# First norm's shift and scale: both vectors through TensorE, in four lots of features

## The chip, the cores and the metric

The kernel runs on one core of one Trainium2 chip. The metric is the device time of one execution in microseconds; of several runs the median is quoted. The engines are TensorE (PE, its weight loads PEld), VectorE (DVE), ScalarE (ACT), GpSimd (POOL) and SyncE (SP), which issues the transfers.

## The reference, cut to what matters

Two layers of a diffusion backbone, on 512 latent tokens `x` and 256 context tokens `ctx` of 1024 features. Each layer is an FFN, a mixer and a second FFN, each between two norms. In front of each of them stands a norm with a shift and a scale, which are vectors made from a conditioning vector (one for latent tokens, one for context):

```python
s_lat, s_ctx = silu(c), silu(c_ctx)[None]
m_l = (s_lat @ w_ada[l] + b_ada[l]).reshape(B, 9, D)   # D = 1024
m_c = (s_ctx @ w_ada[l] + b_ada[l]).reshape(1, 9, D)

def pre_mod(x, g, m, slot):       # slot 0: m[:, 1] is the scale, m[:, 0] the shift
    return rmsnorm(x, g) * (1 + m[:, None, 3 * slot + 1]) + m[:, None, 3 * slot]

def ffn_sublayer(x, m, slot, g_pre, g_post, wg, wu, wd):
    h = pre_mod(x, g_pre, m, slot)
    y = (silu(h @ wg) * (h @ wu)) @ wd
    return post_residual(x, y, g_post, m, slot, 0.5)
```

Shift and scale of layer 0, slot 0 are the first two of the 9 x 1024 columns of `w_ada[0]`. They are needed before the first FFN can start, and the change is about them alone.

## The kernel before, in words

Features lie on the partitions: `X[k]`, k = 0 to 7, holds 128 features of all 768 tokens. Tokens go in three groups: context `G_C` (256), and the latent halves `G_A` and `G_B` (256 each). Every large product is done in three matmuls of rounded numbers: weights and activations are split into a high part and a low part (`whi`/`wlo`, `zh`/`zl`), and `mm3` (lines 515 to 522) adds high x high, high x low and low x high.

The opening is `begin` (line 245), a generator that `ffn` (line 524) advances step by step between its own statements. It loads `G_A`, then lot 0 of the weights, `G_B`, lot 1. A lot `q` is 256 of the 1024 features, that is the two k tiles 2q and 2q+1. For each lot it makes shift and scale, and then the normed tiles `z` of those two k for `G_A` and `G_B` (`z_tile`, line 465: VectorE scales, ScalarE adds the shift and writes `zh` and a full copy into `y`, VectorE or GpSimd subtracts to get `zl`).

- The scale goes through TensorE (line 311): 8 matmuls in f32 with the two silu columns as the stationary operand and 256 weight columns moving, into one bank of 2 x 256. ScalarE copies the row (line 327), two transposes turn it into columns (line 330), VectorE adds the bias and folds in the norm's gain (lines 332, 333).
- The shift goes through VectorE: `ada_dot` (line 243) multiplies transposed weights `wat` (features on the partitions) with `srow`, the silu vectors spread over all partitions, and sums along the row. A lot has two k, two conditioning vectors, and two pieces of each row, so eight dots, each followed by the read of the accumulator; 32 dots in all.

`srow` is made in `consts` (lines 208 to 214) by 16 matmuls of broadcast silu columns with the identity, and four copies. The background vectors of later norms (`ada_bg`, line 353; `pump`) use it too, with the same `ada_dot` on 1024 columns.

The weights of the shift land in `y[0]` to `y[4]` and in the buffers that later hold `gh` and `gl`; those of the scale land in the `raw` ring (four buffers, shared with the FFN's weight tiles) for lots 0 and 3, and in buffers of later z tiles for lots 1 and 2. The transfers are written in pieces: 16 for the shift (rows of 1 to 3 KB) and 10 for the scale (rows of 1 KB).

`ffn` then loads the gate and up tiles of the first two of its 22 feature tiles (`loads(0)`, `loads(1)`, one after lot 0's step, one after lot 1's) and does their products for the latent tokens by k as the z tiles come (`part`, line 676), k 0 to 3, 4 and 5, 6 and 7, then evacuates. After that the context is loaded, normed, and its products done (line 715). `combine` (line 550) forms sums and differences of the normed tokens on VectorE, with which most of the other feature tiles are multiplied (`fast`, line 588).

The order of instructions in each engine's queue is not the order of the text: `TileContext(nc, schedule_with_timeline_sim=True)` has a planner choose it from the dependences, the free buffers, and its own estimate of each instruction's time; the order in the text is the priority. On the chip each engine then takes its queue in order.

Of the kernel before, what the change touches and what calls it, by code (L numbers as in the profile page):

```python
# [5 lines left out]
F32 = mybir.dt.float32  # L6
# [8 lines left out]
P = 128  # L15
# [19 lines left out]
class K:  # L35
# [136 lines left out]
    def consts(self):  # L172
        nc, d = self.nc, self.d
        cp = self.cp = self.pool("const")
        self.sm = self.pool("small")
        cm = cp.tile([P, CM_COLS], F32, name="cm")
        nc.sync.dma_start(cm, d["cm"])
        o = CM_OFF
        self.ident = cm[:, o["ident"] : o["ident"] + P]
        self.LE = cm[:, o["le"] : o["le"] + P]  # L180
        self.GE = cm[:, o["ge"] : o["ge"] + P]
        self.LT = cm[:, o["lt"] : o["lt"] + P]
        self.GT = cm[:, o["gt"] : o["gt"] + P]
        self.C1 = cm[:, o["c1"] : o["c1"] + P]
        self.C2 = cm[:, o["c2"] : o["c2"] + P]
        self.M1 = cm[:, o["m1"] : o["m1"] + 32]
        self.M2 = cm[:, o["m2"] : o["m2"] + 32]
        cols = cp.tile([P, COLS], F32, name="cols")
        nc.sync.dma_start(cols, d["cols"])
        c = lambda n, w, l=0: cols[:, CO[n] + l * w : CO[n] + (l + 1) * w]  # L190
        self.c = c
        self.tab = cp.tile([P, NL], F32, name="tab")
        nc.sync.dma_start(self.tab, d["tab"])
        self.I32 = cp.tile([P, 32], F32, name="i32")
        nc.vector.reduce_sum(self.I32, self.ident.rearrange("p (b c) -> p c b", b=4), axis=AX)
        self.ones = cp.tile([P, P], F32, name="ones")
        nc.vector.memset(self.ones, 1.0)
        self.mhalf = cp.tile([P, 24], F32, name="mhalf")
        nc.vector.memset(self.mhalf, -0.5)
        self.phalf = cp.tile([P, 24], F32, name="phalf")  # L200
        nc.vector.memset(self.phalf, 0.5)
        cs = cp.tile([P, KT, 2], F32, name="cs")
        nc.sync.dma_start(cs, d["cs"])
        self.s = cp.tile([P, KT, 2], F32, name="s")
        nc.scalar.activation(self.s, cs, AF.Silu)
        self.M, self.scol, self.pg = {}, {}, {}

        self.srow = cp.tile([P, 2, 1024], F32, name="srow")
        for v in range(2):
            for h in range(2):  # L210
                ps = self.bank("srow")
                for j in range(4):
                    self.nc.tensor.matmul(ps[:, j * P : (j + 1) * P], self.s[:, 4 * h + j, v : v + 1].to_broadcast([P, P]), self.ident, start=True, stop=True)
                nc.scalar.copy(self.srow[:, v, h * 512 : (h + 1) * 512], ps)


# [20 lines left out]
        self.nc.sync.dma_start(raw, self.d["wat"][l, part, k])  # L237
        return raw

    def ada_dot(self, out, w, v, a, b, start=0.0, keep=False):  # L240

        dst = self.fp.tile([P, 1024], BF16, tag="adot", name="adot", bufs=1)[:, : b - a] if keep else w
        self.nc.vector.tensor_tensor_reduce(out=dst, in0=w, in1=self.srow[:, v, a:b], scale=1.0, scalar=start, op0=ALU.mult, op1=ALU.add, accum_out=out)  # L243

    def begin(self):

# [20 lines left out]
            return r  # L267

        m = {part: self.cp.tile([P, KT, 2], F32, name=f"m0_0_{part}") for part in range(2)}
        sh = self.cp.tile([P, KT, 2], F32, name="sh0")  # L270

        room = list(self.y[:5])
        for j in range(4):
            room += [self.fp.tile([P, NT], F32, tag=f"g{x}{j}", name="land") for x in "hl"]
        KS = [(0, 3), (3, 6), (6, 8)]

        PIECES = [[(0, 0, 768)], [(0, 768, 1024), (1, 0, 512)], [(1, 512, 1024)]]
        w0, w1 = {}, {}

        def load_q(q):  # L280
            cs = lambda part: slice(part * 1024 + q * 256, part * 1024 + (q + 1) * 256)
            for piece in PIECES:
                t, o = room.pop(0), 0
                for j, a, b in piece:
                    w = t[:, o : o + b - a]
                    nc.sync.dma_start(w, self.d["wat"][0, 0, 2 * q + j][:, a:b])
                    w0.setdefault(2 * q + j, []).append((w, a, b))
                    o += b - a
            if q in (1, 2):
                z = 2 * q + 2  # L290
                land = [(a, b, self.zps[q % 2].tile([P, NT], F32, tag=t, name="zland", bufs=1)) for (a, b), t in zip(KS, (f"zh{z}", f"zl{z}", f"zh{z + 1}"))]
            else:
                land = [(a, a + 4, self.wp.tile([P, 1024], F32, tag="raw", name="abraw", bufs=4)) for a in (0, 4)]
            for a, b, t in land:
                w = t[:, : (b - a) * 256].rearrange("p (k c) -> p k c", c=256)
                nc.sync.dma_start(w, self.d["w_ada"][a * P : b * P, cs(0)].rearrange("(k p) c -> p k c", p=P))
                for k in range(a, b):
                    w1[q, k] = w[:, k - a]

        load_x(G_A)  # L300
        load_q(0)
# [2 lines left out]
        yield  # L304
        for q in range(4):
            d = slice(2 * q, 2 * q + 2)
            ps = self.bank("adaps")
            if 0 < q < 3:
                load_q(q + 1)
            for k in range(KT):  # L310
                nc.tensor.matmul(ps[0:2, 0:256], self.s[:, k], w1[q, k], start=k == 0, stop=k == KT - 1)
            for k in (2 * q, 2 * q + 1):
                for v in range(2):
                    start = 0.0
                    for w, a, b in w0[k]:
                        self.ada_dot(sh[:, k, v : v + 1], w, v, a, b, start, keep=v == 0)
                        start = sh[:, k, v : v + 1]
            if q == 0:
                squares(G_A)
                squares(G_B)  # L320
            if q in (1, 2):
                z = 2 * q + 2
                self.zh[z] = self.zps[q % 2].tile([P, NT], F32R, tag=f"zh{z}", name=f"zh{z}", bufs=1)
                self.zl[z] = self.zps[q % 2].tile([P, NT], F32R, tag=f"zl{z}", name=f"zl{z}", bufs=1)
                self.zh[z + 1] = self.zps[q % 2].tile([P, NT], F32R, tag=f"zh{z + 1}", name=f"zh{z + 1}", bufs=1)
            row = self.sg("row")[0:2, 0:256]
            nc.scalar.copy(row, ps[0:2, 0:256])
            pt = self.aux("adapt")
            for j in range(2):
                nc.tensor.transpose(pt[:, 2 * j : 2 * j + 2], row[:, j * P : (j + 1) * P], self.ident[0:2, 0:2])  # L330
            b = lambda part: self.c("b_ada", KT, part)[:, d].unsqueeze(2).to_broadcast([P, 2, 2])
            nc.vector.tensor_tensor(out=m[1][:, d], in0=pt[:, 0:4].rearrange("p (d v) -> p d v", v=2), in1=b(1), op=ALU.add)
            nc.vector.scalar_tensor_tensor(out=m[1][:, d], in0=m[1][:, d], scalar=1.0, in1=self.c("norm_pre", KT, 0)[:, d].unsqueeze(2).to_broadcast([P, 2, 2]), op0=ALU.add, op1=ALU.mult)
            nc.vector.tensor_tensor(out=m[0][:, d], in0=sh[:, d], in1=b(0), op=ALU.add)
            if q == 0:
                self.M[0, 0, 0], self.M[0, 0, 1] = m[0], m[1]
                self.scol[0, 0] = m[1]
                R = {g: factor(g) for g in (G_A, G_B)}
            for g in (G_A, G_B):
                for k in (2 * q, 2 * q + 1):  # L340
                    self.z_tile(0, 0, g, R[g], k)
            yield
        load_x(G_C)

        def rest():
            squares(G_C)
# [6 lines left out]
    def ada_bg(self, l, slot, parts, vecs):  # L353


        raw = self.cp.tile([P, 3, KT, 2], F32, name=f"raw{l}_{slot}_{parts[0]}")

        def col(pi, k, w):
            for v in vecs:
                self.ada_dot(raw[:, pi, k, v : v + 1], w, v, 0, 1024, keep=v != vecs[-1])  # L360

        def fin():
            if len(vecs) == 1:
                self.nc.vector.tensor_copy(raw[:, : len(parts), :, 1], raw[:, : len(parts), :, 0])
            self.ada_cols(l, slot, raw, parts)

        for pi, part in enumerate(parts):
            for k in range(KT):
                dma = lambda a=(l, 3 * slot + part, k): self.ada_dma(*a)
                self.bg.append((dma, lambda w, a=(pi, k): col(*a, w)))  # L370
        self.bg.append((None, fin))
# [1486 lines left out]
def pack(i):  # L1858
# [4 lines left out]
    o["x"] = A(np.stack([xt[:, :, g[0] : g[0] + g[1]].transpose(1, 0, 2) for g in GROUPS]))  # L1863
    o["cs"] = A(np.stack([i["c"][0], i["c_ctx"]], -1).reshape(KT, P, 2).transpose(1, 0, 2))

    o["w_ada"] = A(i["w_ada"][0, :, 1024:2048])
    o["wat"] = A(i["w_ada"].transpose(0, 2, 1).reshape(2, 9, KT, P, 1024))
    T = lambda a, w: a.reshape(-1, w, P).transpose(2, 0, 1).reshape(P, -1)
    cols = dict(
# [146 lines left out]
```

## Time and profile before

| | us |
|---|---|
| median of 3 runs | 3329.84 |
| lowest, highest | 3324.64, 3330.06 |
| the profiled execution | 3321.82 |
| its span, first to last instruction | 3320.0 |

TensorE is busy 3058.4 us of the span, VectorE 2562.9, ScalarE 1377.4 and GpSimd 1345.7. All times in the rows below count from the start of the span. In rows of a timeline the first two numbers are the start and the duration, x8 is a run of eight merged instructions, and in brackets stands the idle time of the engine before it with what ended it. In windows the numbers of each engine are its busy time, then come the granted clock of TensorE as a share of 2.4 GHz (0.50 is 1.2 GHz), the busy share of the transfer engines and what they moved. In rows of groups a bar separates shape and count from the busy time, the mean of one in ns, and the idle time before.

### The profile page before, as it was taken

The page shows a single profiled execution, that of the slowest core. Times are in us where ns is not written, and L with a number is a line of the kernel's source. Part 1 is how long each engine was busy: PE and PEld are TensorE (multiplying, and loading weights), DVE is VectorE, ACT ScalarE, POOL GpSimd, SP SyncE. Part 2 cuts the span into 40 slices and gives each one's busy share as a digit, 9 for nine tenths or more (in the row PEclk, how much of TensorE's full clock was granted, in tenths as well). Part 3 has the DMA queues.
Part 4 walks back from the last instruction along what each step waited for, and adds up shares of the span by engine and source line. Part 5 has one row for each costly group of instructions (what it writes and reads, how often), then busy time and mean ns, then how long its engine had stood idle before and what let it go on. Part 6 is the DMA issues. An engine that isn't in the chain of part 4 may idle for free. (4 is left out here: it accounts for less than half of the span.)

```text
span 3320.0 us, 53695 instructions
## 1 busy us (share of the span) xinstructions
PE 3058.4 (92%) x20836; PEld 2785.7 (84%) x20836; DVE 2562.9 (77%) x4337; ACT 1377.4 (41%) x2600; POOL 1345.7 (41%) x1060
## 2 busy tenths in 40 slices
PE   7899999889889998999998899999989788989998
PEld 4799989878787798999998798999877676788998
DVE  7888887777778959677777977777677879776777
ACT  4333223544445644322234432223454346544343
POOL 5322122544655765222215511221544546753233
PEclk8999999889999899999999999999989899989999
DMA  6233333222310122323324233332322310224233
GB/s 221 101 122 122 107 127 117 94 73 54 97 64 10 51 86 81 108 91 107 101 73 158 82 109 114 121 127 89 104 98 64 88 46 17 91 90 134 96 106 98
DMA packets 149816, 318.68 MB, mean 96 GB/s; under 512 B 38185, under 2 KB 79529, under 8 KB 149561
## 3 DMA queue, kind: packets, MB, share of 16 engines
q1 hardware_dynamic: 149560, 315.25, 28.9%
q8 instruction: 163, 2.67, 0.3%
q14 instruction: 93, 0.75, 0.1%
HBM read 285.17 MB, written 30.03 MB: 95 GB/s over the span
## 5 line engine op out<-in xcount | busy, mean ns | idle before, releaser
L94 POOL TENSOR_TENSOR wlo<-wraw,whi 128x1024 fp32r<-128x1024 f32 (+1 forms) x228 | 580.3, 2554 | 1357.5 <-ACT whi L93 1304.9
L93 ACT CAST whi<-wraw 128x1024 fp32r<-128x1024 f32 (+2 forms) x482 | 469.5, 978 | 692.0 <-PE ps L776 338.5
L519 PE MATMUL ps<-zh,whi 128*128 128x256 f32 (+1 forms) x1208 | 389.5, 331 | 25.2 <-DVE sg L547 13.3
L608 PE MATMUL ps<-zh,whi 128*128 128x384 f32 (+1 forms) x1216 | 392.2, 323 | 8.0 <-DVE sg L547 4.5
L609 PE MATMUL ps<-zl,whi 128*128 128x384 f32 (+1 forms) x1216 | 392.1, 322 | 2.5 <-DVE zl L586 2.5
L610 PE MATMUL ps<-zh,wlo 128*128 128x384 f32 (+1 forms) x1216 | 390.8, 322 | 0.0
L520 PE MATMUL ps<-zl,whi 128*128 128x256 f32 (+1 forms) x1208 | 382.9, 327 | 5.0 <-DVE zl L477 5.0
L775 PE MATMUL ps<-gh,whi 128*128 128x512 f32 (+1 forms) x1008 | 349.5, 354 | 21.3 <-ACT gh L618 18.9
L776 PE MATMUL ps<-gl,whi 128*128 128x512 f32 (+1 forms) x1008 | 338.3, 352 | 17.3 <-DVE gl L619 17.3
L522 PE MATMUL ps<-zh,wlo 128*128 128x256 f32 (+1 forms) x1208 | 351.1, 324 | 0.0
L94 DVE TENSOR_TENSOR wlo<-wraw,whi 128x1024 fp32r<-128x1024 f32 (+1 forms) x254 | 298.1, 1175 | 31.3 <-ACT whi L93 29.9
L778 PE MATMUL ps<-gh,wlo 128*128 128x512 f32 (+1 forms) x1008 | 293.3, 348 | 0.0
L519 PEld LDWEIGHTS ps<-zh,whi 128*128 128x128 f32 x1208 | 236.8, 199 | 56.8 <-DVE sg L547 14.0
L520 PEld LDWEIGHTS ps<-zl,whi 128*128 128x128 f32 x1208 | 238.3, 198 | 24.5 <-DVE zl L477 6.1
L775 PEld LDWEIGHTS ps<-gh,whi 128*128 128x128 f32 x1008 | 191.7, 192 | 65.2 <-ACT gh L618 21.8
L608 PEld LDWEIGHTS ps<-zh,whi 128*128 128x128 f32 x1216 | 229.4, 189 | 10.9 <-ACT whi L93 4.8
L243 DVE CUSTOM_DVE_ANT_0 abraw<-abraw,srow 128x1024 f32<-128x1024 f32 x128 | 208.0, 1625 | 33.2 <-DMA abraw<-in_wat 31.2
L776 PEld LDWEIGHTS ps<-gl,whi 128*128 128x128 f32 x1008 | 193.5, 192 | 46.7 <-DVE gl L619 19.6
L609 PEld LDWEIGHTS ps<-zl,whi 128*128 128x128 f32 x1216 | 229.5, 189 | 3.5 <-DVE zl L586 3.2
L610 PEld LDWEIGHTS ps<-zh,wlo 128*128 128x128 f32 x1216 | 229.4, 189 | 0.0
L522 PEld LDWEIGHTS ps<-zh,wlo 128*128 128x128 f32 x1208 | 222.4, 199 | 6.5 <-issue 1.0
L243 DVE CUSTOM_DVE_ANT_0 adot<-abraw,srow 128x1024 bf16<-128x1024 f32 x96 | 151.3, 1576 | 63.2 <-DMA abraw<-in_wat 62.8
(394 smaller groups left out, 7722.3 us busy)
## 6 DMA issues: line engine op xcount, KB each, us to landing
wraw<-in_wu SPq DMA_DIRECT2D x176, 512.0 KB, 3.3
abraw<-in_wat SPq DMA_DIRECT2D x128, 512.0 KB, 3.3
wraw<-in_wd SPq DMA_DIRECT2D x88, 512.0 KB, 3.5
wraw<-in_wi SPq DMA_DIRECT2D x44, 512.0 KB, 3.4
wraw<-in_wo SPq DMA_DIRECT2D x16, 512.0 KB, 4.0
xs<-x SPq DMA_DIRECT2D x64, 128.0 KB, 1.7
x<-xs SPq DMA_DIRECT2D x64, 128.0 KB, 3.4
x<-in_x SPq DMA_DIRECT2D x48, 128.0 KB, 3.7
```

Source lines behind the costliest of these rows:

```text
L93: nc.scalar.copy(hi[:, :n], raw[:, :n])
L94: (eng or nc.gpsimd).tensor_sub(lo[:, :n], raw[:, :n], hi[:, :n].bitcast(F32))
L243: self.nc.vector.tensor_tensor_reduce(out=dst, in0=w, in1=self.srow[:, v, a:b], scale=1.0, scalar=start, op0=ALU.mult, op1=ALU.add, accum_ ...
L519: nc.tensor.matmul(ps, wh, self.zh[k][:, off : off + n], start=first, stop=False)
L520: nc.tensor.matmul(ps, wh, self.zl[k][:, off : off + n], start=False, stop=False)
L522: nc.tensor.matmul(ps, wl, self.zh[k][:, off : off + n], start=False, stop=last)
L608: nc.tensor.matmul(ps, w[0][:, c], xh, start=k == 0, stop=False)
L609: nc.tensor.matmul(ps, w[0][:, c], xl, start=False, stop=False)
L610: nc.tensor.matmul(ps, w[1][:, c], xh, start=False, stop=k == 3)
L775: nc.tensor.matmul(ps, wh[:, o : o + P], gh[j][:, off : off + n], start=j == 0, stop=False)
L776: nc.tensor.matmul(ps, wh[:, o : o + P], gl[j][:, off : off + n], start=False, stop=False)
L778: nc.tensor.matmul(ps, wl[:, o : o + P], gh[j][:, off : off + n], start=False, stop=j == nf - 1)
```

## The change

The shift takes the path of the scale. The host lays both parts of the weights out by lots: `w_ada[q]` is 128 partitions x 4096, one row of 16 KB for each partition, in which unit `u = 2k + part'` (scale first) is the 256 columns of k tile k. A lot is loaded in four transfers of four units (lot 0) or six of at most three units. Each lot lands in a place of its own: lot 0 in the four `raw` buffers, lot 1 in six buffers of `gh` and `gl`, lots 2 and 3 in the z tiles and the `y` tiles of their own two k. Lots 0 and 1 are loaded at the start, lot q+2 in the step of lot q. For each lot two banks take 16 matmuls, two row copies and four transposes follow, then the same three vector instructions. `srow` moves from `consts` into `rows()`, which `begin` calls after its last lot, behind the load of `G_C`.

```diff
+    def rows(self):
+        nc = self.nc
+        self.srow = self.cp.tile([P, 2, 1024], F32, name="srow")
...
-    def ada_dot(self, out, w, v, a, b, start=0.0, keep=False):
+    def ada_dot(self, out, w, v, keep=False):
...
+        zt = lambda x, k: self.zps[0 if k > 5 else 1].tile([P, NT], F32, tag=f"z{x}{k}", name="zland", bufs=1)
+        unit = {}
+        def land(q):
+            if q == 0:
+                return [self.wp.tile([P, 1024], F32, tag="raw", name="abraw", bufs=4) for _ in range(4)]
+            if q == 1:
+                return [self.fp.tile([P, NT], F32, tag=f"g{x}{j}", name="land") for j in range(3) for x in "hl"]
+            return [zt(x, k) for k in (2 * q, 2 * q + 1) for x in "hl"] + [self.y[2 * q + 1], self.y[2 * q]]
         def load_q(q):
...
+            tiles, n = land(q), 4 if q == 0 else 3
+            for i, t in enumerate(tiles):
+                us = range(i * n, min(i * n + n, 16))
+                nc.sync.dma_start(t[:, : len(us) * 256], self.d["w_ada"][q][:, us[0] * 256 : (us[-1] + 1) * 256])
+                for u in us:
+                    unit[q, u] = t[:, (u - us[0]) * 256 : (u - us[0] + 1) * 256]
...
         for q in range(4):
-            ps = self.bank("adaps")
-            if 0 < q < 3:
-                load_q(q + 1)
+            ps = [self.bank("adaps") for _ in range(2)]
+            if q < 2:
+                load_q(q + 2)
             for k in range(KT):
-                nc.tensor.matmul(ps[0:2, 0:256], self.s[:, k], w1[q, k], start=k == 0, stop=k == KT - 1)
-            for k in (2 * q, 2 * q + 1):
-                for v in range(2):
-                    start = 0.0
-                    for w, a, b in w0[k]:
-                        self.ada_dot(sh[:, k, v : v + 1], w, v, a, b, start, keep=v == 0)
-                        start = sh[:, k, v : v + 1]
+                for part in range(2):
+                    nc.tensor.matmul(ps[part][0:2, 0:256], self.s[:, k], unit[q, 2 * k + part], start=k == 0, stop=k == KT - 1)
...
-            row = self.sg("row")[0:2, 0:256]
-            nc.scalar.copy(row, ps[0:2, 0:256])
             pt = self.aux("adapt")
-            for j in range(2):
-                nc.tensor.transpose(pt[:, 2 * j : 2 * j + 2], row[:, j * P : (j + 1) * P], self.ident[0:2, 0:2])
+            for part in range(2):
+                row = self.sg("row")[0:2, 0:256]
+                nc.scalar.copy(row, ps[part][0:2, 0:256])
+                for j in range(2):
+                    c = 4 * part + 2 * j
+                    nc.tensor.transpose(pt[:, c : c + 2], row[:, j * P : (j + 1) * P], self.ident[0:2, 0:2])
...
-            nc.vector.tensor_tensor(out=m[0][:, d], in0=sh[:, d], in1=b(0), op=ALU.add)
+            nc.vector.tensor_tensor(out=m[0][:, d], in0=w(0), in1=b(0), op=ALU.add)
...
         load_x(G_C)
+        self.rows()
...
-    o["w_ada"] = A(i["w_ada"][0, :, 1024:2048])
+    o["w_ada"] = A(i["w_ada"][0, :, :2048].reshape(KT, P, 2, 4, 256)[:, :, ::-1].transpose(3, 1, 0, 2, 4).reshape(4, P, 4096))
```

## Rows read from the trace of the kernel before

**Rows 1.** The page: the span, and TensorE's busy tenths in 40 slices.

```profile
span 3320.0 us, 53695 instructions
...
PE   7899999889889998999998899999989788989998
```

**Rows 2.** Windows of the opening, ten microseconds each, all engines.

```profile
0.00:10.00 10.00, 3.79 (x18) 3.79 (x18) 0.60 (x4) 4.55 (x10) 2.99 (x8) 1.00 0.76 241
10.00:20.00 10.00, 7.70 (x32) 3.95 (x31) 6.21 (x17) 4.06 (x9) 5.04 (x7) 0.83 0.99 333
20.00:30.00 10.00, 6.94 (x26) 3.32 (x26) 8.87 (x24) 4.91 (x11) 6.12 (x6) 0.75 1.00 354
30.00:40.00 10.00, 6.88 (x26) 2.46 (x24) 9.93 (x19) 2.78 (x7) 6.93 (x4) 0.84 1.03 366
```

**Rows 3.** Timeline of TensorE from 14 to 80 us.

```profile
14.82 5.29 PE L311 MATMUL adaps<-abraw,s 128*2 128x256 f32 x16 [2.30 <-DMA abraw<-in_w_ada]
...
24.70 2.38 PE L311 MATMUL adaps<-zland,s 128*2 128x256 f32 x6 [0.92 <-DMA zland<-in_w_ada]
...
43.16 0.39 PE L520 MATMUL ps<-zl,whi 128*128 128x512 f32 x1
43.39 0.40 PE L522 MATMUL ps<-zh,wlo 128*128 128x512 f32 x1
...
49.28 0.79 PE L520 MATMUL ps<-zl,whi 128*128 128x512 f32 x1 [3.04 <-DVE zl L477]
...
61.19 1.89 PE L311 MATMUL adaps<-abraw,s 128*2 128x256 f32 x8
...
67.77 0.28 PE L330 MATMUL adapt<-cm,row 2*128 2x2 f32 x2
67.98 0.61 PE L155 MATMUL rb<-ones,be 128*128 128x1 f32 x4
69.90 0.71 PE L165 MATMUL rb<-cm,rbr 128*128 128x128 f32 x4 [1.32 <-POOL rbr L159]
71.90 1.28 PE L519 MATMUL ps<-zh,whi 128*128 128x512 f32 x4 [1.29 <-ACT zh L472]
...
79.33 0.28 PE L520 MATMUL ps<-zl,whi 128*128 128x256 f32 x1
```

**Rows 4.** Windows of line 243 alone, the sum over 0 to 80 us.

```profile
sum 80.00, DVE 37.43; mean DVE 9.36
```

**Rows 5.** Groups of instructions, 0 to 80 us: the background dots.

```profile
L243 DVE CUSTOM_DVE_ANT_0 adot<-abraw,srow 128x1024 bf16<-128x1024 f32 x2 | 4.6, 2290 | 1.3 <-DMA abraw<-in_wat 1.3
...
L243 DVE CUSTOM_DVE_ANT_0 abraw<-abraw,srow 128x1024 f32<-128x1024 f32 x2 | 2.7, 1336 | 0.4 <-issue 0.2
```

**Rows 6.** Timeline of TensorE, SP's queue and VectorE, 0 to 70 us.

```profile
6.21 6.31 PE L213 MATMUL srow<-cm,s 128*128 128x128 f32 x32 [6.21 <-ACT s L205]
...
34.06 6.95 SPq L256 DMA_DIRECT2D x<-in_x  x8
...
41.12 0.93 SPq L296 DMA_DIRECT2D abraw<-in_w_ada  x2
...
60.82 3.36 DVE L243 CUSTOM_DVE_ANT_0 adot<-abraw,srow 128x1024 bf16<-128x1024 f32 x1 [0.82 <-DMA abraw<-in_wat]
```

**Rows 7.** Windows of the opening: TensorE's list, and two stretches of its clock.

```profile
12.50:79.30 66.80, 52.68 (x195) 30.29 (x195) 60.63 (x126) 31.91 (x74) 39.63 (x34) 0.85 0.66 227
16.00:18.00 2.00, 2.00 (x6) 0.65 (x5) 1.66 (x7) 1.30 (x4) 0.39 (x1) 0.50 1.04 327
26.00:28.00 2.00, 2.00 (x8) 1.10 (x7) 2.00 (x5) 1.25 (x4) 0.43 (x1) 0.50 1.03 410
```

**Rows 8.** Window of the stage behind the context's products.

```profile
111.00:150.00 39.00, 28.43 (x134) 24.77 (x135) 34.53 (x52) 12.52 (x24) 13.13 (x5) 0.87 0.47 162
```

**Rows 9.** Waits from 110 to 150 us: total, times, longest.

```profile
PE ps L609 <- DVE zl L586: 2.5, 2, 1.8
PE ps L608 <- DVE sg L547: 2.4, 1, 2.4
```

More of the change, by code (lines that the diff above doesn't have):

```diff
@@ L212, in consts @@
                 for j in range(4):
-                    self.nc.tensor.matmul(ps[:, j * P : (j + 1) * P], self.s[:, 4 * h + j, v : v + 1].to_broadcast([P, P]), self.ident, start=True, stop=True)
+                    nc.tensor.matmul(ps[:, j * P : (j + 1) * P], self.s[:, 4 * h + j, v : v + 1].to_broadcast([P, P]), self.ident, start=True, stop=True)
                 nc.scalar.copy(self.srow[:, v, h * 512 : (h + 1) * 512], ps)
@@ L238, in ada_dma @@
         return raw
-    def ada_dot(self, out, w, v, a, b, start=0.0, keep=False):
-        dst = self.fp.tile([P, 1024], BF16, tag="adot", name="adot", bufs=1)[:, : b - a] if keep else w
-        self.nc.vector.tensor_tensor_reduce(out=dst, in0=w, in1=self.srow[:, v, a:b], scale=1.0, scalar=start, op0=ALU.mult, op1=ALU.add, accum_out=out)
+    def ada_dot(self, out, w, v, keep=False):
+        dst = self.fp.tile([P, 1024], BF16, tag="adot", name="adot", bufs=1) if keep else w
+        self.nc.vector.tensor_tensor_reduce(out=dst, in0=w, in1=self.srow[:, v], scale=1.0, scalar=0.0, op0=ALU.mult, op1=ALU.add, accum_out=out)
     def begin(self):
@@ L269, in begin @@
         m = {part: self.cp.tile([P, KT, 2], F32, name=f"m0_0_{part}") for part in range(2)}
[L270 to L278, printed above, removed]
-        def load_q(q):
[L281 to L298, printed above, removed]
@@ L320, in begin @@
                 squares(G_B)
[L321 to L325, printed above, removed]
-            row = self.sg("row")[0:2, 0:256]
-            nc.scalar.copy(row, ps[0:2, 0:256])
-            pt = self.aux("adapt")
-            for j in range(2):
-                nc.tensor.transpose(pt[:, 2 * j : 2 * j + 2], row[:, j * P : (j + 1) * P], self.ident[0:2, 0:2])
+            if q > 1:
+                for k in (2 * q, 2 * q + 1):
+                    self.zh[k], self.zl[k] = (self.zps[3 - q].tile([P, NT], F32R, tag=f"z{x}{k}", name=f"z{x}{k}", bufs=1) for x in "hl")
+            pt = self.aux("adapt")
+            for part in range(2):
[4 more added lines that the diff above has]
+                    nc.tensor.transpose(pt[:, c : c + 2], row[:, j * P : (j + 1) * P], self.ident[0:2, 0:2])
             b = lambda part: self.c("b_ada", KT, part)[:, d].unsqueeze(2).to_broadcast([P, 2, 2])
-            nc.vector.tensor_tensor(out=m[1][:, d], in0=pt[:, 0:4].rearrange("p (d v) -> p d v", v=2), in1=b(1), op=ALU.add)
+            w = lambda part: pt[:, 4 - 4 * part : 8 - 4 * part].rearrange("p (d v) -> p d v", v=2)
+            nc.vector.tensor_tensor(out=m[1][:, d], in0=w(1), in1=b(1), op=ALU.add)
             nc.vector.scalar_tensor_tensor(out=m[1][:, d], in0=m[1][:, d], scalar=1.0, in1=self.c("norm_pre", KT, 0)[:, d].unsqueeze(2).to_broadcast([P, 2, 2]), op0=ALU.add, op1=ALU.mult)
-            nc.vector.tensor_tensor(out=m[0][:, d], in0=sh[:, d], in1=b(0), op=ALU.add)
+            nc.vector.tensor_tensor(out=m[0][:, d], in0=w(0), in1=b(0), op=ALU.add)
             if q == 0:
@@ L359, in col @@
             for v in vecs:
-                self.ada_dot(raw[:, pi, k, v : v + 1], w, v, 0, 1024, keep=v != vecs[-1])
+                self.ada_dot(raw[:, pi, k, v : v + 1], w, v, keep=v != vecs[-1])
         def fin():
```

1 line of the change is left out of this document (removed).

## The prediction

> **What bounds the kernel now.** I read the page first. TensorE is busy in nearly every slice of the span but the first [rows 1]; the change touches only the opening, so that is where I look. Next come windows of ten microseconds. From 10 to 40 us the transfer engines are full (share 0.99 to 1.03) and move 3.3 to 3.7 MB in each; VectorE fills up too (8.87, then 9.93 of 10), while TensorE is busy about 7 of 10 [rows 2]. Third, TensorE's timeline. It starts the first lot's vectors at 14.82 and waits 0.92 us for weights before the second lot; at 49.28 it has waited 3.04 us for VectorE; the last lot's vectors run to 63, the last shares of the first two weight tiles start at 71.90, and the context's products (256 columns) start at 79.33 [rows 3]. 79.33 is the milestone of this prediction: up to there all is opening, and behind it TensorE is dense for thirty microseconds. Last, what filled VectorE. All of line 243 takes 37.43 us in the first 80 [rows 4]; 4.6 and 2.7 of it are the background vectors, which stay [rows 5]. So some 30 us are the dots of the shift. The z tiles queue among them on VectorE, and TensorE waits for the z tiles.
>
> **What goes.** The 32 dots with their accumulator reads, 30 us of VectorE between 11 and 59. That is not 30 us of time: TensorE and the transfers have bounds of their own.
>
> **What is added on TensorE.** Each of these matmuls shows as two records, so a lot has 16 now (8 k, one part) and 32 after (8 k, two parts): 128 in all instead of 64. Eight took 1.89 us at the full clock, 0.236 each, and 64 more are 15.1 us; six took 2.38 in a stretch at half clock, 0.40 each, which would make it 25 [rows 3]. The results take two banks and two row copies for a lot instead of one, and four transposes instead of two, at 0.28 us for two [rows 3]; the copies fall to ScalarE, which is busy less than half of 10 to 40 us [rows 2].
>
> **The new floor of the opening.** TensorE's list up to the milestone: 128 x 0.236 = 30.2 us of vectors; 96 products of 512 columns (two tiles, gate and up, 8 k, three each) which start 0.23 apart, 22.1; three rounds of statistics at 0.61 + 0.71, 4.0; 16 transposes, 2.2 [rows 3]. Together 58.5. The list can't start ahead of the first weights. Constants (0.97 MB by their shapes), the first x group (1.05) and a quarter of lot one (0.52) make 2.54 MB, where 2.41 were moved by 10 us [rows 2]: 10.4. TensorE is then still on the silu rows, until 12.5 (below). The floor is 12.5 + 58.5 = 71.0 against 79.3: no more than 8.3 us can be won here.
>
> **Transfers.** The bytes are the same, the order is not. Adding up (a lot 2.10 MB, an x group 1.05, a pair of weight tiles 1.05) against 2.41, 5.74, 9.28 and 12.94 MB at 10, 20, 30 and 40 us [rows 2]: lot one is in at 15.1, lot two at 24.3, lot three at 30.2, the first weight tiles at 33.1, lot four at 38.8. TensorE needs 7.6 us for a lot (32 x 0.236), so from lot two on it is behind the transfers. Now the last lot's scale is asked for only at 41.12, when its buffers come free [rows 6]; with a place of its own it waits for none. In exchange the first weight tiles are queued on SP behind the six loads of lot three, and must wait for lot one to leave the four raw buffers: 10.41 MB stand up to their end instead of 8.31, 33.1 us instead of 27.3. Behind them on SP stand lot four and the second tiles, and GpSimd's low parts wait for them. TensorE has lot three's vectors to do until then, 7.6 us from about 27, so I cost the 6 us at nothing; without that cover they would count in full. Longer rows could raise the rate; I take nothing for it.
>
> **Moved: the silu rows.** 32 records, 6.31 us at 6.21 [rows 6], and four copies on ScalarE; no transfer goes with them. In the text they now stand behind the last evacuation of the first two tiles. But the engines' queues don't follow the text: the context's x is asked for at 34.06, ahead of the last lot at 41.12, and the first background dot runs at 60.82, ahead of the last z tiles [rows 6], each written later than what it overtook. The rows need only the silu and the identity, and TensorE has nothing else before 10.4. I expect them at about 6 us still and take 0. Run where they are written they cost 6.3 behind the milestone, and hold back the background dots; at the other end 1 to 2 us are won, if lot one overtakes them.
>
> **Waits and clock.** Between 12.5 and 79.3 TensorE is busy 52.68 of 66.8 us at a mean clock of 0.85 [rows 7]: 14.1 us of waits; and the list of before at full clock (42.3) is 10.4 under the busy time, which is the half speed. The waits for VectorE should go; those for the first landings, for statistics and for row copies stay in part. Of the 14.1 I keep 2, of the half speed 1.5, which puts the milestone at 74.5: 4.8 won. The ends are none of it and all of it.
>
> The clock is where a rule speaks against the change. The rows: TensorE stands at 1.2 GHz (0.50) from 16 to 18 and from 26 to 28 us, both soon after a wait for weights, though it is busy all of either stretch [rows 7]. The Trainium skill ("TensorE: Matmul & The Clock Gate", section "HAM oscillation — how this bites in real kernels") says that a thin matmul which waits for every transfer is throttled anew at each, and advises against the shape; the two stretches agree. By it the sum would be that of the slow rival below.
>
> **Behind the milestone.** From 111 to 150 us TensorE idles 10.6 of 39 us while VectorE is busy 34.5 [rows 8], and the waits for line 586 and line 547 name VectorE [rows 9]. VectorE comes to the context and the combinations with no slack now; of its 60.63 us between 12.5 and 79.3 [rows 7] the change leaves about 31, so it should lead TensorE there. Against it, the two early background vectors (7.3 us) may slip into this stage. I take 3 won; the ends are 7.3 lost and 10.6 won.
>
> **Sum.** 4.8 + 3 = 7.8, call it 8 us. The profiled execution took 3321.82 (a span of 3320.0 [rows 1] and 1.8 around it), so 3314 by its own account. The median of the three runs is 3329.84, 8 us above it, and the runs lie up to 5.4 apart. On the median: 3322.
>
> **Rivals.**
> 1. *More:* the milestone at its floor (8.3) and the stage behind it freed of much of its idle time: 11 to 18 won, 3312 to 3319. For it: the long waits of both stretches name VectorE. Against: the transfers, and GpSimd's low parts of the weight tiles, are not relieved. 0.15.
> 2. *Nothing that shows:* TensorE keeps half of its waits, or the silu rows run late (6.3): 5 won to 4 lost, 3325 to 3334. For it: TensorE takes its queue in order, and each lot still goes through matmul, copy, transpose, vector work and z tile. Against: the longest waits were for an engine that is now relieved. 0.22.
> 3. *Slower:* TensorE runs the vectors of three lots at half clock. A record then costs 0.40 for 0.236, so the 8.3 are gone after 50 of the 128 records, which is the point from which it decides; with 96 at half clock 15.7 are lost. Net 8 lost, up to 15 with the old waits kept: 3337 to 3345. For it: both stretches at 0.50. Against: they came behind idle time on TensorE, which now has twice the work for the same landings. 0.15.
> 4. *Forecast:* 5 to 11 won, 3319 to 3325. 0.48.
>
> **Numbers.** About 0.2% (6.7 us) is what a measurement of this kernel can tell from no change. Faster by more: rival 1 and three quarters of the forecast, 0.15 + 0.36 = 0.51. Same: the rest of the forecast and rival 2, 0.12 + 0.22 = 0.34. Slower: rival 3, 0.15. The range leaves out rival 3 and little else, 3312 to 3334; within it the forecast alone has 3319 to 3325.
>
> **What would show it.** Right, if the lots' matmul has 128 records at a step near 0.24; if VectorE is under 6 of 10 from 20 to 50 us; if the silu rows stand at 6 us, the context's first product near 74, and the work that is now at 150 near 142. Wrong, if the clock reads 0.5 through the middle lots (rival 3), if TensorE's waits move to row copies and z tiles (rival 2), or if the milestone comes early and the lead is gone by 150.

## The result, and the profile after

The changed kernel takes 3348.24 us, the median of 4 runs (3340.63 to 3350.24), beside 3329.46 us for the kernel before (4 runs, 3324.64 to 3330.06): a ratio of 1.0055, 95% interval 1.0037 to 1.0074. It is slower by 18.8 us, outside the predicted 3312 to 3334. Its profiled execution took 3347.67. Three executions far above the others (9863 us of run 1, 11559 us of run 12, 4215 us of the kernel before in runs 13 to 15) are left out of the medians below, as they are of the ratios.

The page after, against [rows 1]: the span, and TensorE's busy tenths.

```profile
span 3345.8 us, 53771 instructions
...
PE   7899999889899998999998899999989798989998
```

The span is 25.8 us longer, and no slice of TensorE stands out. Windows of the opening after, against [rows 2] (TensorE, its weight loads, VectorE, ScalarE, GpSimd; granted clock; share of the transfer engines, GB/s):

```profile
10.00:20.00 10.00, 7.29 (x23) 2.47 (x24) 0.00 (x0) 2.75 (x7) 4.30 (x7) 1.00 0.97 327
20.00:30.00 10.00, 10.00 (x50) 4.23 (x48) 0.52 (x4) 1.88 (x5) 3.76 (x6) 1.00 1.01 365
30.00:40.00 10.00, 9.23 (x49) 4.36 (x48) 4.45 (x9) 4.79 (x11) 6.09 (x4) 1.00 1.03 401
40.00:50.00 10.00, 9.49 (x42) 4.93 (x43) 6.50 (x12) 8.50 (x20) 5.82 (x5) 1.00 0.73 241
...
70.00:80.00 10.00, 6.20 (x44) 5.53 (x43) 8.41 (x20) 4.47 (x11) 1.67 (x1) 0.95 0.09 19
80.00:90.00 10.00, 9.73 (x45) 8.48 (x45) 9.81 (x20) 7.76 (x19) 5.44 (x6) 0.71 0.26 88
```

VectorE is nearly free from 10 to 30 us, TensorE is busy from 20 on, and the clock reads 1.00 throughout. The opening does what was forecast, up to 70 us, but for the first lot (below). TensorE's timeline after, against [rows 3] and [rows 6]:

```profile
12.71 9.41 PE L305 MATMUL adaps<-abraw,s 128*2 128x256 f32 x32 [12.71 <-DMA abraw<-in_w_ada]
...
65.93 0.83 PE L216 MATMUL srow<-cm,s 128*128 128x128 f32 x6
...
72.08 3.06 PE L216 MATMUL srow<-cm,s 128*128 128x128 f32 x26
74.98 0.50 PE L155 MATMUL rb<-ones,be 128*128 128x1 f32 x4
77.59 0.71 PE L165 MATMUL rb<-cm,rbr 128*128 128x128 f32 x4 [2.11 <-POOL rbr L159]
80.27 1.65 PE L509 MATMUL ps<-zh,whi 128*128 128x256 f32 x5 [1.96 <-ACT zh L462]
```

The silu rows (L216) did not go to 6 us. They run from 65.93 and from 72.08, ahead of the context's statistics (L155) in TensorE's queue. GpSimd had finished the sum of squares that these need long before, and VectorE then has four background dots, released by the rows, in front of the context's z:

```profile
58.64 4.13 POOL L395 TENSOR_TENSOR be<-be,bt 128x256 f32<-128x256 f32 x5
...
74.48 1.23 DVE L246 CUSTOM_DVE_ANT_0 adot<-abraw,srow 128x1024 bf16<-128x1024 f32 x1
...
78.05 1.22 DVE L246 CUSTOM_DVE_ANT_0 abraw<-abraw,srow 128x1024 f32<-128x1024 f32 x1
...
79.19 1.26 DVE L459 SCALAR_TENSOR_TENSOR bt<-x,m,rb 128x256 f32<-128x256 f32 x3
```

So the milestone is 80.27 instead of 79.33, and behind the waits the clock of 80 to 90 us is 0.71. The stage behind it, against [rows 8] and [rows 9], by window and by waits:

```profile
111.00:150.00 39.00, 26.00 (x126) 23.77 (x125) 35.41 (x47) 11.71 (x19) 13.69 (x5) 0.87 0.43 149
```

```profile
PE ps L598 <- ACT whi L93: 6.6, 1, 6.6
PE ps L765 <- DVE c L633: 3.2, 1, 3.2
PE ps L766 <- DVE gl L609: 3.2, 1, 3.2
```

VectorE is no freer there than before (35.41 us of 39, 34.53 then), and TensorE idles 13.0 us instead of 10.6. Its longest wait names ScalarE, but leads to VectorE: the cast of `whi` had itself waited 7.57 us for VectorE's work on the weights in line 588.

```profile
120.31 1.04 ACT L93 CAST whi<-wraw 128x1024 fp32r<-128x1024 f32 x1 [7.57 <-DVE wraw L588]
```

Where the rest went is seen by matching matmuls. For each statement I took the starts of its matmuls in both traces, in order, and subtracted; the medians of these offsets to the kernel before, in us, by stretch of time:

```
                           180-200  600-700  1000-1200  2000-2200  2800-3000  end
after                          6.4      9.7        9.2       13.8       23.4  25.4
```

About 6 us come from the opening. 19 more come in a drift behind it, most of it behind 1200 us, in stages whose text the change does not touch. That is one execution of each kernel: before's lies 7.6 us under its median, the change's 0.6, so that by medians some 12 of the 19 are left.

### The profile page after: what moved, and what is told of

It reads as the page before. It is cut to its first block, busy times and chain, and to the rows that moved or that the text cites. A ratio compares the mean times of both kernels' runs of the same rounds, so it can differ in the third digit from the quotient of the medians.

```text
span 3345.8 us, 53771 instructions
## 1 busy us (share of the span) xinstructions
PE 3087.6 (92%) x20908; PEld 2809.9 (84%) x20908; DVE 2532.5 (76%) x4273; ACT 1379.5 (41%) x2604; POOL 1348.4 (40%) x1060
## 5 line engine op out<-in xcount | busy, mean ns | idle before, releaser
L768 PE MATMUL ps<-gh,wlo 128*128 128x512 f32 (+1 forms) x1008 | 300.0, 354 | 0.0
L509 PEld LDWEIGHTS ps<-zh,whi 128*128 128x128 f32 x1208 | 239.3, 202 | 53.0 <-DVE sg L537 12.5
L598 PE MATMUL ps<-t42h,whi 128*128 128x384 f32 (+1 forms) x608 | 197.7, 325 | 7.1 <-ACT whi L93 7.1
```

The costliest lines, as they stand in the source:

```text
L509: nc.tensor.matmul(ps, wh, self.zh[k][:, off : off + n], start=first, stop=False)
L598: nc.tensor.matmul(ps, w[0][:, c], xh, start=k == 0, stop=False)
L768: nc.tensor.matmul(ps, wl[:, o : o + P], gh[j][:, off : off + n], start=False, stop=j == nf - 1)
```

## The experiments

Call the time from the start of a matmul to the start of the next its step. The steps show what drifts: matmuls of 256 and 384 columns whose moving operand lies on the left of SBUF (`gh`, `gl`, and the `t42` and `t` tiles, which hold the sums of `combine`) step more slowly, and those that move `zh` or `zl` against weights hardly do (under 1 ns). Some 360 that move `zh` or `zl` against a stationary `gh` or `gl` slow down as well, from 114 or 115 to 119 ns (last section). The change dropped the tile `sh0`, 64 bytes a partition, and with it every later tile on the left moved down by 64 bytes. The theory "address" was put against "rows" (the late silu rows) in the first four runs. Before took 3329.75 in these.

**1. The change with 64 bytes put back.** All queues in the same order as in the change, but for the one memset.

```diff
+        pad = self.cp.tile([P, 16], F32, name="pad")
+        nc.gpsimd.memset(pad, 0.0)
```

> The changed kernel with one unused tile of 64 bytes where the old kernel had the shift's tile, so that every tile of the left pools stands at its old address; all queues keep their order but for one memset. Address theory (the loss behind the opening, 19 of 25 us, is matmuls that read their moving operand at an address shifted by 64 bytes): about 3329 us, ratio to the kernel before 0.999 to 1.003, the step of the 256-column products on gh and gl back from 121 ns to 113-118. Order theory (the loss is the planner's new order, or anything else the 64 bytes don't touch): 3348 us, ratio 1.0055.

Measured: 3338.48 us, ratio 1.0029 (1.0017 to 1.0041), 9.8 less than the change. "Address" holds, at half the size that the steps had promised; neither expected time came. In the traces run 1 and the change are level at 180 to 200 us (6.5 and 6.4 behind before) and 15.4 apart at the end (10.0 and 25.4); run 1's profiled execution, 3331.78, lies 6.7 us under its median.

**2. The kernel before, moved by 64 bytes** with the same two lines; all queues in the order of before.

> The kernel before with one more unused tile of 64 bytes, so that the tiles of the left pools move by 64 bytes and stand in the same place modulo 128 as in the changed kernel; the queues keep their order. Address theory: 15 to 20 us slower than the kernel before, ratio 1.0045 to 1.006, with no change in the opening. Order theory: no change, ratio 1.000.

Measured: 3334.47 us, 1.0016 (1.0007 to 1.0024). An unused tile costs an untouched kernel 5 us, a third of the 15 to 20 expected.

**3 and 4. The silu rows early again**, without and with the 64 bytes.

```diff
         self.M, self.scol, self.pg = {}, {}, {}
+        self.rows()
...
         load_x(G_C)
-        self.rows()
```

> The changed kernel with the silu rows made in consts again, at the start. Theory of the opening (the rows, late in TensorE's queue and ahead of the context's statistics, cost it some 8 us at the context's first product): 6 to 9 us faster than the changed kernel, near 3340 us, ratio 1.003, context's first product near 72 us instead of 80. Rival (the opening is limited elsewhere, the rows only fill a gap): within 2 us of the changed kernel, 3346 to 3350. Addresses are those of the changed kernel.

> Silu rows at the start and the 64-byte tile together. If both theories hold and their prices add up: 3348 - 19 - 8 = 3321 us, ratio 0.996 to 0.999, so faster than the kernel before. If only the addresses hold: 3329, ratio 1.000. If only the rows hold: 3340, ratio 1.003.

Measured: 3348.00 (1.0065, 1.0051 to 1.0079) and 3336.56 (1.0029, 1.0018 to 1.0040). TensorE's timeline of run 3:

```profile
6.10 5.97 PE L217 MATMUL srow<-cm,s 128*128 128x128 f32 x32 [6.10 <-ACT s L205]
...
12.98 7.07 PE L306 MATMUL adaps<-abraw,s 128*2 128x256 f32 x32 [0.91 <-DMA abraw<-in_w_ada]
...
74.96 1.27 PE L509 MATMUL ps<-zh,whi 128*128 128x256 f32 x5 [1.85 <-ACT zh L462]
```

The milestone is at 74.96, 4.4 us ahead of before, yet nothing of it is left at the end. "Rows" explains the opening and not the end: run 3 missed the 6 to 9 us that it was to win, and run 4 the three times that were put down for it. The next thing to suspect is the order: the planner writes all queues anew when the opening changes. With the last 93% of each queue compared with before's, TensorE's order differs in 56 places in the change and in run 1, and in 98 places in runs 3 and 4.

**5 and 6. Two more places for the tiles of the kernel before:** `zh` and `zl` 64 bytes lower (a tile of 16 columns in front of the weight pool), and the left tiles 96 bytes higher (the lines of run 1 with 24 columns); TensorE, VectorE, ScalarE and SP in before's order. Before took 3328.24 in runs 5 to 8.

```diff
         self.wp = self.pool("w", side="right")
+        self.nc.gpsimd.memset(self.wp.tile([P, 16], F32, name="wpad"), 0.0)
```

> The kernel before with 64 unused bytes in front of the weight pool on the right, so that the tiles zh and zl lie 64 bytes lower (their offset modulo 128 goes from 96 to 32, the place that gh, gl and the t tiles have in the kernel before); every queue keeps its order. Theory 'address': a matmul whose moving operand lies at 96 modulo 128 pays more; then the steps of the 256-column products of zh and zl fall from 120 ns to 113 to 117, on about 3,660 of them, so 10 to 20 us less: 3310 to 3320. Rival 'left only': what cost the time was something else that moved on the left (sums, x, small tiles), and zh and zl don't care: within 3 us of before.

> The kernel before with 96 unused bytes on the left: the left tiles go from 32 to 0 modulo 128; every queue keeps its order. Theory 'address' with a period of 128 leaves two cases: 0 is as good as 32 (within 2 us of before, 256-column steps of gl at 114 to 117 ns) or as bad as 96 (+5 us, as the run that moved them by 64, steps at 120 to 121). Rival, 'any move costs': +5 us again with no pattern.

Measured: 3326.66 (0.9996, 0.9987 to 1.0004) and 3333.13 (1.0012, 1.0003 to 1.0021). In run 5 the 256-column steps of `zl` against weights fell from 124.5 to 120.0 ns on average, as "address" says; those of `zl` against `gh` rose from 115.1 to 120.6, and the 384-column ones of the `t` tiles, of which no operand had moved, by 1.1 to 2.1 ns. The time stayed: the expected 10 to 20 us did not come. Run 6 is 4.9 us over before, which "as bad as 96" and "any move costs" had both allowed.

**7. Another order for the kernel before.** One thin matmul more for each lot.

```diff
+            px = self.bank("px")
+            nc.tensor.matmul(px[0:2, 0:256], self.s[:, 0], w1[q, 0], start=True, stop=True)
```

> The kernel before with one thin matmul more for each lot (four in all, into a bank that nobody reads; eight records of 0.236 us, 2 us of TensorE in the opening). All addresses stay; but the planner's order of the queues behind the opening changes in 94 places on TensorE. Theory 'order': what remains of the loss when the addresses are restored (9 us by medians, of which the opening shows only 1 to 6.5) is the order that the planner chose anew; then this kernel, with an order much like the one of the run with early rows, ends 5 to 12 us later though its opening is 2 us later at most, and the offset to before grows in jumps between 700 and 2500 us. Rival 'opening': the order is worth nothing, and it ends 0 to 3 us later.

Measured: 3339.69, 1.0035 (1.0023 to 1.0048). Four thin matmuls cost 11.5 us. The time is in the range of the theory "order", but by another way: the opening was 7.1 us late by 180 us, where 2 at most had been expected (why was not taken apart), and 4.4 came behind it.

**8. The change with the 64 bytes and the rows behind lot 1.**

```diff
+            if q == 1:
+                self.rows()
             yield
         load_x(G_C)
-        self.rows()
```

> The changed kernel with the 64 bytes restored and the silu rows written behind lot 1: the same work and the same addresses as e1_pad and e4_rows_early_pad, a third order of the queues. Theory 'order': the end isn't tied to the opening: it differs from e1_pad (3338.7) and e4_rows_early_pad (3336.6) by several us, either way. Rival 'opening': the offset that it has to before at 180 us, expected between those two (1 to 6.5), stays to the end, and the median is 3331 to 3336.

Measured: 3334.11, 1.0016 (1.0007 to 1.0024). TensorE fills its opening, by windows and timeline:

```profile
20.00:30.00 10.00, 10.00 (x56) 4.90 (x53) 0.52 (x4) 2.06 (x6) 4.11 (x6) 1.00 1.02 384
...
60.00:70.00 10.00, 10.00 (x50) 8.12 (x49) 7.35 (x16) 3.51 (x9) 6.62 (x6) 1.00 0.33 107
```

```profile
13.11 8.48 PE L307 MATMUL adaps<-abraw,s 128*2 128x256 f32 x32 [13.11 <-DMA abraw<-in_w_ada]
...
76.05 0.97 PE L512 MATMUL ps<-zh,whi 128*128 128x256 f32 x5 [1.40 <-ACT zh L465]
```

The median lies in the range of the rival "opening", but not for its reason: the run is 2.1 us ahead of before at 180 to 200 us and ends behind. Its opening does not carry to the end, as the order theory has it; that it is the order which takes it is not shown by this run.

**9. Run 8 with `zh` and `zl` 64 bytes lower**, by the line of run 5, in run 8's order. Before took 3329.50 in runs 9 to 12.

> The changed kernel with the 64 bytes restored, the silu rows behind lot 1 (3334.1 in its own run) and, new, zh and zl 64 bytes lower; the same order of all queues as the run with the rows behind lot 1. Theory 'address': the 256-column products of zh and zl step 3 to 5 ns less and the 384-column ones 1 ns more, as in the kernel before, which is a few us less: 3328 to 3333, at best level with before. Rival: no change, 3334.

Measured: 3329.12, 1.0003 (0.9994 to 1.0012): 5 less than run 8 by medians, as expected, 4 by the ratios, whose intervals overlap.

**10 to 12. The silu rows split**, the 64 bytes in place: `rows` takes a list of (vector, half), and its four parts are called in the constants, behind lot 0, 0 and 1 (run 10), behind lot 1 and three times behind the context's load (run 11), in the constants, behind lot 0, 3 and 3 (run 12). Same work and addresses, three orders.

```diff
+        self.rows([(0, 0)])
...
-    def rows(self):
+    def rows(self, vh):
...
+        for v, h in vh:
...
+            self.rows({0: [(0, 1), (1, 0)], 1: [(1, 1)]}.get(q, []))
             yield
```

> The changed kernel with the 64 bytes restored; the four silu rows written one at a time (one in the constants, two behind lot 0, one behind lot 1). Same work, same addresses; this makes the planner's order behind the opening the same as that of the kernel before up to some 600 us and from 800 to 2300 us. Theory 'order': the offset to before at 180 us is -2 to 2 us, stays flat over the stretches of equal order, and the loss of the others (7 to 11 us behind the opening) shrinks: 3328 to 3333. Rival 'opening': something that the change does in the opening costs 5 to 9 us later whatever the order: 3334 to 3339.

> The changed kernel with the 64 bytes restored; one silu row behind lot 1, the other three behind the load of the context. Same work, same addresses; the order of all queues is that of the kernel before from about 1000 us to the end. Theory 'order': the offset to before is 3 to 6 us at 180 us (three rows late), changes between 600 and 1000 us where the orders differ, and is flat behind it, within 1 us: 3331 to 3336. Rival: it goes on growing behind 1000 us as in the runs before (2 to 9 us there).

> The changed kernel with the 64 bytes restored; one silu row in the constants, one behind lot 0, two behind lot 3. Same work, same addresses, another order in nearly every stage (58 places on TensorE). Theory 'order': its end is not tied to its opening (offset at 180 us expected between 0 and 4): anywhere from 3327 to 3340, with jumps where the orders differ. Rival 'opening': the offset at 180 us stays: 3329 to 3333.

Measured: 3329.70 (1.0004, 0.9995 to 1.0013), 3341.94 (1.0041, 1.0028 to 1.0053) and 3338.66 (1.0036, 1.0022 to 1.0049). Run 10, whose order is nearest to before's after run 11's, is level with before. Run 11 missed its expectation twice: its opening was 9.5 us late, because its three late rows stood ahead of the context's statistics again, and its offset grew from 12.8 to 20.6 us behind 1000 us although the order there is before's. So not all of an offset is order. Before's own profiled execution is 7.6 us under its median of 3329.46, and the excess of run 11's last offset over the difference of the medians (20.6 less 12.4) is 8.2: a drift against that one execution overstates by about so much.

All runs that have before's addresses, with the places on TensorE where the order differs from before, the offset at 180 to 200 us, the median against the median of before in the same runs, and what is left:

```
run                      places  offset at 180-200  median - before  left
10 rows split c001           37               -0.0              0.2   0.2
11 rows split 1444           24                9.5             12.4   3.0
1  change with 64 bytes      56                6.5              8.7   2.2
12 rows split c033           58                2.9              9.2   6.3
8  rows behind lot 1         88               -2.1              5.9   8.0
7  before, other order       94                7.1             11.5   4.4
4  rows early                98                0.9              6.8   5.9
```

The three orders nearest to before's (24 to 56 places) leave 0.2 to 3.0 us, the other four (58 to 98) 4.4 to 8.0. With intervals of 3 to 5 us to either side of a median this puts the cost of an order between nothing and 8 us, and does not say which places cost it.

**13 to 15. The addresses with the order held.** Run 10 with `zh` and `zl` lower; run 10 without the 64 bytes; before with 192 bytes on the left (48 columns). Before took 3329.64.

> The run with the split silu rows (c001, 3329.7, level with before) with zh and zl 64 bytes lower, the order of all queues held. Theory 'address': as with the rows behind lot 1 (3334.1 to 3329.1), 2 to 5 us less: 3325 to 3328, which would be the fastest of all. Rival: the gain of the 256-column steps is given back elsewhere: 3328 to 3331.

> The run with the split silu rows without the 64 bytes restored, so that the left tiles lie where the change put them; the order of all queues held. Theory 'address': 8 to 11 us more than with them: 3337 to 3341; the steps of the 256-column products of gl go from 113 to 120 ns, and those of the 384-column t products from 173 to 175 or 176. Rival 'order': the addresses cost only 4 to 5 us, as in the kernel before moved by 64, and the rest was the order: 3333 to 3335.

> The kernel before with 192 unused bytes on the left: the left tiles go to 96 modulo 256, the changed kernel's place, where the run moved by 64 was at 224; the order of all queues held. A period of 256: the 384-column t products step at 175 to 177 ns, 9 to 11 us more: 3338 to 3341. A period of 128: 173.6 ns, 5 us more: 3333 to 3336.

Measured: 3325.42 (0.9992, 0.9983 to 1.0001), 3335.77 (1.0018, 1.0009 to 1.0027) and 3337.76 (1.0027, 1.0016 to 1.0037). With the order held the 64 bytes cost 6.1 us (run 14 less run 10; 4.7 by the ratios, whose intervals just overlap), between the ranges of "address" (8 to 11) and of its rival (4 to 5), while the steps moved as "address" says (`gl` 116.1 to 120.3 ns, `t` of 384 columns 173.1 to 176.5). The same place modulo 256 costs the kernel before 8.1. Run 13 has the lowest median of all, 22.8 us under the change; against before its interval reaches 1.0001, so it is not shown to be faster than before.

The groups of one tile show the place directly (duration in ns, least/median/most, first and last start, forms). The down products that move `gl`, 352 matmuls of 256 columns (the form is counted on every second one), in the kernel before, in the change, in run 1, and in run 15:

```profile
L805 PE MATMUL ps<-gl,whi x352: 276/276/415, 573.6 to 3302.3; 128*128 128x256 f32 x176
```

```profile
L795 PE MATMUL ps<-gl,whi x352: 274/282/287, 582.5 to 3328.1; 128*128 128x256 f32 x176
```

```profile
L797 PE MATMUL ps<-gl,whi x352: 276/276/282, 582.9 to 3312.3; 128*128 128x256 f32 x176
```

```profile
L807 PE MATMUL ps<-gl,whi x352: 279/282/290, 578.0 to 3315.0; 128*128 128x256 f32 x176
```

And `zl` in the mixer's products, run 10 and then run 13, where only `zh` and `zl` moved:

```profile
L511 PE MATMUL mixp<-zl,whi x128: 278/283/580, 616.8 to 2408.3; 128*128 128x256 f32 x128
```

```profile
L512 PE MATMUL mixp<-zl,whi x128: 276/276/583, 617.3 to 2418.0; 128*128 128x256 f32 x128
```

The reader is to see 276 against 282 or 283, the same instruction on the same form, switched in both directions by the place of tiles: of all left tiles in the first four lines, of `zh` and `zl` alone in the last two.

## Why the prediction was wrong

**What went, what was added, the floor: right.** VectorE's busy time from 10 to 60 us, the sum of five windows, fell from 45.0 to 16.0 us: 29, where the dots of the shift were put at 30; only its last sign of this, under 6 of 10 up to 50 us, was missed by the window from 40 (6.50). 128 records were there; in run 8 24 of them took 5.34 us, 0.22 each, where 0.236 was taken. The forecast put the milestone at 74.5 with the silu rows early: run 3, which has them early, shows 74.96.

**Transfers: right, at the start by luck.** The first weights let TensorE start at 12.71, where 12.5 had been forecast for another reason: the silu rows were to keep TensorE busy until then. The landing itself, estimated at 10.4, came 2.3 us later. From 20 to 70 us it was busy 9.23 us or more of every ten, so the queue in front of the first weight tiles cost nothing.

**Waits and clock: right but for the first lot.** The windows read 1.00 in every ten microseconds up to 70, but the trace has no record of the clock before 17.48 us: the first eleven records of the change step 0.427 us, the others of the lot 0.216, as at the lower and the higher level. TensorE had done nothing for the 12.71 us before. In run 3 the silu rows ran in front, and the same 32 records all step 0.216 (7.07 us for the lot instead of 9.41). It cost little: lot two starts at 21.95 in the change and, waiting for its weights, at 21.22 in run 3. Rival 3 did not happen. The Trainium skill's rule that spoke for it ("TensorE: Matmul & The Clock Gate", section "HAM oscillation — how this bites in real kernels") is about a thin matmul that waits for each transfer, and after the first lot the change's TensorE waited for none; the runs leave it untested. The median lies beyond rival 3's 3337 to 3345, by other mechanisms.

**Moved: the silu rows: the first step that failed.** "I expect them at about 6 us still and take 0" was wrong: they ran at 65.93 and 72.08. The bracket had the price right ("6.3 behind the milestone, and hold back the background dots"); run 3 against the change gives it as 6.5 us at 180 to 200 us. Rival 2 had this case, with 4 us lost at most. That the context's loads and dots had overtaken older work was read as a rule of this planner, and it is none: these four rows stayed about where they were written.

**Behind the milestone: the second step that failed.** Plus 3 us were taken for a VectorE that leads TensorE. Run 3 reached the milestone 4.4 us ahead and was level at 180 to 200 us: 4.3 lost in place of 3 won, within the bracket (7.3 lost) and on its wrong side. It still led by 2.5 us from 120 to 140 us and lost that by 150, in the very stage that was to add to it (one of the signs of being wrong that the prediction names):

```profile
111.00:150.00 39.00, 27.85 (x131) 25.04 (x132) 35.96 (x53) 12.44 (x20) 14.23 (x5) 0.82 0.48 162
```

The 29 us freed lie ahead of the milestone, where the dots stood. Behind it VectorE has as much to do as before, 35.96 us of 39 in run 3 and 35.41 in the change against 34.53. That this work is released by the context's products and the evacuations, and so could not be done ahead, is how the text of the kernel reads; no run tried it.

**The sum: what failed most was a term that was not in it.** The sum ended at 150 us and let the rest of the kernel stand. The removal of the tile `sh0` goes with the change, and was costed as nothing. By experiment it costs 6.1 us with the order held (run 14 against run 10), 8.1 on the kernel before (run 15) and 9.8 in the change itself (run 1); by the ratios 4.7, 9.0 and 8.7. The order anew, behind the opening, leaves 2.2 us in run 1, whose order is the change's; it is the remainder and not measured alone. Of the 18.5 us that the change lies over before's 3329.75, 6.5 are then opening (run 1's offset), 9.8 addresses and 2.2 order; with a remainder in it, such a sum comes out whatever the cause. The first two are shown; that the third is order is argued, and it carries the error of all.

The theory "address" was itself over-sized: the longer steps of the change add up to 19 us over 180 to 3320 us, and the medians show 6 to 10. The traced executions of the change and of run 1 are 15.9 us apart (3347.67 and 3331.78), so part of the gap is that an execution below its median was traced; where the rest is hidden stays open. A reason at hand is that TensorE waits elsewhere for VectorE and ScalarE, and a longer step shortens the wait; this was not tried.

## What to carry to other kernels

When a change adds or drops a tile, even an unused one of 64 bytes, first compare the step of a few untouched matmuls far from the change: a drift there can be the allocator's work, and a pad that restores the addresses shows it before the change is judged. Where a planner writes the queues, ask of a moved piece of work where it will stand, and not what it depends on; and hold the order, or vary it several times, before a difference of 0.2% is laid to the change. The time freed on VectorE helped here only the opening, in which its work had stood, so a lead has to be looked for in the stage that is to use it.

## What the runs showed of the hardware that was not expected

The step of a matmul on rounded f32 (f32r) depends on the byte offsets of its operands in a partition. Mean start-to-start times in ns, by the moving operand, with weights at 224 modulo 256 as the stationary one, 180 to 3320 us, steps under 300 ns, by kernel and the offset of the left tiles modulo 256 (all large tiles of a side share it):

```
                     before  +64 (run 2)  +96 (run 6)  +192 (run 15)  change (-64)
offset mod 256          160          224            0             96            96
gl, 256 columns       116.8        121.7        119.3          120.1         120.9
t42 low, 256 columns  115.5        120.0        116.7          119.1         119.0
t42 high, 384 columns 172.9        173.8        173.6          176.4         176.6
gl, 512 columns       234.7        229.8        233.2          232.2         232.0
```

Run 15 and the change, 256 bytes apart, agree in every row within 0.8 ns, while runs 2 and 15, 128 apart, differ by 2.6 ns at 384 columns and 2.4 at 512: the period is 256 bytes and not 128, as far as five places can tell. No place is best for all widths: 160 is best for 256 and 384 columns and worst for 512. `zl`, moved from 224 to 160 in run 5, gained 4.5 ns at 256 columns and lost 0.5 at 384, against weights.

The moving operand's place is not all of it. Where `gh` or `gl` is the stationary operand (in `ps<-zl,gh` the first is moved, the second stationary), the move of `zl` from 224 to 160, which gained above, loses: run 10, then run 13.

```profile
L511 PE MATMUL ps<-zl,gh x120: 276/276/365, 1198.0 to 2930.7; 128*128 128x256 f32 x120
```

```profile
L512 PE MATMUL ps<-zl,gh x120: 280/283/363, 1197.4 to 2938.8; 128*128 128x256 f32 x120
```

And where only the stationary operand moves, `gl` with the other left tiles from 160 to 96, the same befalls a `zh` that stays: the kernel before, then run 15.

```profile
L522 PE MATMUL ps<-zh,gl x120: 276/276/280, 1198.8 to 2931.0; 128*128 128x256 f32 x120
```

```profile
L524 PE MATMUL ps<-zh,gl x120: 278/281/287, 1199.1 to 2941.9; 128*128 128x256 f32 x120
```

By the traces the steps at 256 columns go with the distance of the two: 64 bytes apart they are the shortest of their kind (`gl` at 160 against weights at 224, 116.8 ns; `zl` at 224 against `gh` at 160, 115.1; `zh` at 224 against `gl` at 160, 113.6), at the same place modulo 256 they are 121.7, 120.6 and 120.0, and 128 apart (`gl` at 96 against weights, `zh` against `gl` at 96) 120.1 and 118.8. That is read off these runs and was not tested by one of its own, and the distance does not explain the `t` tiles of 384 columns, whose steps rose by 1 to 2 ns in run 5 with both operands in place.

The Trainium skill ("SBUF — State Buffer", section "Operand start alignment") asks only that an operand start at a multiple of its element size, and says of its measurements "these runs timed nothing"; all places here satisfy it, and they differ by up to 5 ns in 117. What in the chip makes the difference was not found.
